# A delta-rule layer's exponentials and powers reordered, pooled sums on zero-padded rows, small parameters loaded one group ahead

## The chip, the cores and the metric

The kernel runs on one core of one Trainium2 chip. The metric is the device time of one execution in microseconds. Engine names in the profile: PE is TensorE (PEld its weight loads), DVE is VectorE, ACT is ScalarE, POOL is GpSimd, SP is SyncE, which here only issues DMAs.

## The reference

A decoder trunk of four pre-norm residual layers on x of 256 tokens by 1024 channels, all in float32, with one last RMSNorm. The layers are, in order: pooling mixer, gated delta rule, latent attention, pooling mixer. What matters here is cut from the reference:

```python
def pool_mixer(h, w_in, w_grp, scale, w_out):            # layers 0 and 3
    u, gate = jnp.split(h @ w_in, 2, axis=-1)            # 2 x 2048 channels
    ...                                                  # groups of 512 channels, windows 2, 4, 8, 16
        mean = (cg[:, 1:] - lo) / cnt                    # causal mean over w tokens, cnt = min(t + 1, w)
        groups.append(mean.astype(u.dtype) - u[..., sl])
    p = jnp.einsum('bsgi,gio->bsgo', p, w_grp)...
    y = p * scale * jax.nn.silu(gate)
    return y @ w_out

def gdn_mixer(h, w_in, conv_w, a_log, dt_bias, norm_g, w_out):   # layer 1
    proj = h @ w_in
    qkv = jax.nn.silu(causal_depthwise_conv(qkv, conv_w))        # 4 taps
    q = l2norm(q) * (GDN_DK ** -0.5);  k = l2norm(k)             # x * rsqrt(sum(x * x) + EPS)
    beta = jax.nn.sigmoid(b_raw)
    g = -jnp.exp(a_log) * jax.nn.softplus(a_raw + dt_bias)
    o = chunk_gated_delta_rule(q, k, v, g, beta)
    o = rmsnorm(o, norm_g) * jax.nn.silu(gate)
    return o @ w_out

def chunk_gated_delta_rule(q, k, v, g, beta):
    g = jnp.cumsum(g, axis=-1)
    decay = jnp.exp(jnp.where(causal, g_i - g_j, -jnp.inf))
    L = jnp.where(strict, (k_beta @ k^T) * decay, 0.0)
    sol = triangular_solve(I + L, [v_beta, k_beta * exp(g)])     # unit lower triangular
    attn = jnp.where(causal, (q @ k^T) * decay, 0.0)
    ...                                                          # a state is carried from chunk to chunk
```

## The kernel before, in words

**Products.** Every large product is made of float32 values split into two parts of fewer bits, a high and a low one: `weights` loads a piece of 128 x 1024 of a weight matrix into one of three buffers `raw` (SP's queue), ScalarE casts it to `whi` (L149, L153) and VectorE subtracts to get `wlo` (L150, L154; a few pieces on GpSimd, by the argument `pool`). Both go to a ring of nine buffers. PE then makes three matmuls (high by high, high by low, low by high) at L162. `project` runs eight k-steps of 128 rows for 512 columns into PSUM banks named `acc` (or `aux`).

**Order of the work.** The program is written in an order by hand, and a planner then orders each engine's queue by due times from its own model of costs. Each engine works through its queue strictly in order, so a step that waits holds everything behind it on that engine. `later(*instructions)` makes the steps traced inside it come after the given instructions on the engine of each of these, and adds no wait between engines. `mark` keeps the last instruction of a kind for that.

**Pool layer** (`pool_layer`, layers 0 and 3). Four groups in the order 3, 2, 1, 0; for each, `gate(g)` and `pooled(g)`; the product with the group's weights, `mixed`, follows one group later. `pooled` brings the projection to a tile `u` (128 channels x 4 x 256 tokens), and then builds window sums by doubling: level `lev` adds a copy shifted by d = 2^lev tokens. The first d columns have no partner and are copied on GpSimd (L552), the rest is a sum on VectorE (L553). L557 corrects the first tokens' counts, L561 forms `p`, and L242 and L247 split it to `ph` and `pl` for `mixed`.

**Small parameters.** After the gates of the first layer's groups 3, 2 and 1 stand `turn_params` with `window_counts`, `gdn_setup` and `mla_setup`. Each loads small parameters on ScalarE's queue and uses them at once: `turn_params` transposes the gains' rows on PE (L489) to `colsT`; `gdn_setup` transposes the convolution's taps (L640, L641) and splits the small weights `bw` to `bws` (L647, L648); `mla_setup` makes the position tables by some twenty small VectorE steps (L1108 on).

**Delta-rule layer** (`gdn_layer`). The order by hand is

```python
order = "g0 k0 d a0 k1 a1 s g1 q0 v0 v1 v2 b q1 i V3 c3 g2 u0 u1 g3".split()
```

where g is a gate's projection (512 columns), k a half of the keys, q a half of the queries, v a quarter of the values, and:

- Before the loop, the cumulated g of each token is made (`G`), turned, written to DRAM and read back to every partition as `Gb` (GpSimd's queue, L730, L733); 16 VectorE steps (L740) form `DT` = min(Gb - G, mask).
- d, `decays`: the exponentials of both halves of `DT`, of `Eb` (= `Gb[1]`) and of `eG` on ScalarE (L748).
- k and q, `channels`: projection, convolution (`conv`: four scalings on ScalarE, L755, and 12 steps on VectorE, L758), silu on ScalarE (L804), transposes on PE (L810), squares on ScalarE (L813), their sum `ssq` on VectorE (L814). `keys` then makes on GpSimd `ssq` + EPS (L841) and `rk`, its power -1/2 (L789), and on VectorE `s1` = rk * beta (L843), `s2` = s1 * rk (L845).
- a, `lower`: k by k^T on PE (L823), times s2 and the decay on VectorE, giving `LT` (L832); diagonal blocks of 32 are copied out (L856, L858).
- s, `substitution`: VectorE turns the blocks (L861), GpSimd solves them by 31 pairs of steps (L867, L871). Also the reciprocal `rki` = 1 / rk (L873), by which the values are scaled (L934).
- b, `blocks_back`: VectorE turns the result (L878), ScalarE and GpSimd copy it to the blocks of `T` (L885, L887), and GpSimd scales the token-wise keys `ktok` (L888).
- i, `inverses`: the 32-blocks are joined to inverses of 64. V3, c3 and u: last values, and the first chunk's new values.
- `queries` ends with a product on VectorE (L902) and, on GpSimd after the last substitution step (mark "blocks"), the powers of the queries' norms (L904 to L908). They are used by `output` (L1060, L1063), `ktok` by `state` (L1029).

ScalarE's functions lie in tables; a change between exponential, logarithm and silu shows in the profile as an ACT_TABLE_LOAD at the line of the next function.

## Time and profile before

| | |
|---|---|
| time, median of 3 runs | 816.21 us (813.97 to 816.85) |
| time of the profiled execution | 817.07 us |
| its span, first to last instruction | 815.4 us |
| mean granted TensorE clock | 0.992 |
| instructions | 16122 |
| GpSimd busy | 148.7 us (18%) |
| read from HBM | 136.74 MB, 169 GB/s over the span |

A row of the profile names the line, the engine, the operation, the tile written and those read (out<-in), the shape and the count. In a timeline the two numbers ahead are the start and the duration in us, and the bracket at the end is the time for which the engine was idle before, and what it waited for. Rows of groups end in the total busy time and the mean duration in ns of one. "Busy" of PE counts pipelined matmuls, so a busy PE need not be at its peak. "Granted clock" is the share of full speed that PE's clock had.

### The profile page before, as it was taken

The numbers are of one execution on the slowest core, as the hardware profiler recorded it, in microseconds if no ns is written. First come the engines' busy times: TensorE is split into PE (matmuls) and PEld (weight loads), VectorE is DVE, ScalarE is ACT, GpSimd is POOL, SyncE is SP. The second block draws the span as 40 slices with busy tenths as digits, with TensorE's granted clock in tenths as the row PEclk, the third lists the DMA queues.
The fourth block names the chain that finished last, engine by engine and source line by source line (L and its number), as shares of the span: only waits on it lengthen the run. The fifth ranks groups of instructions, "written<-read, shape, count | busy, mean of one in ns | idle before, by whom it ended". The sixth has DMA issues, their size and how long they took to land.

```text
span 815.4 us, 16122 instructions
## 1 busy us (share of the span) xinstructions
PE 794.6 (97%) x5966; PEld 754.8 (93%) x5966; DVE 598.6 (73%) x1133; ACT 500.2 (61%) x1009; POOL 148.7 (18%) x292
## 2 busy tenths in 40 slices
PE   8989999999989989999999999999999999999996
PEld 7979999989889988888989999999999989999996
DVE  4699987667889976456677659778877667877863
ACT  6566555567876855455565654566655575566662
POOL 3001100233037852022212013000000210000011
PEclk9999999999999999999999999999999999999999
DMA  6765666746455633323557686753652646676562
GB/s 208 227 177 177 197 214 219 219 154 209 152 161 156 205 113 100 127 73 108 182 148 221 204 191 183 208 145 87 182 172 74 187 153 196 191 222 207 198 213 53
DMA packets 106615, 138.85 MB, mean 170 GB/s; under 512 B 19044, under 2 KB 48936, under 8 KB 106536
## 3 DMA queue, kind: packets, MB, share of 16 engines
q1 hardware_dynamic: 104032, 136.07, 55.2%
q0 software_dynamic: 320, 1.06, 0.4%
q8 instruction: 47, 0.77, 0.4%
q10 hardware_dynamic: 2184, 0.69, 0.4%
q14 instruction: 32, 0.26, 0.1%
HBM read 136.74 MB, written 1.06 MB: 169 GB/s over the span
## 4 chain that ended last, share of the span: by engine, by line
PE 85%; POOL 5%; ACT 3%; DVE 3%; issue 2%; DMA 1%; ACTq 0%; SPq 0%; DVEq 0%; POOLq 0%
PE acc L162 69%; PE aux L162 8%; POOL X L867 2%; POOL U L871 2%; ACT whi L149 1%; PE tp L1337 1%; DVE cv L758 1%; DMA x<-in_x_dram 1%; DVE wlo L150 1%; PE aux L823 1%; ACT junk L256 1%; PE tp L419 0%; PE aux L979 0%; PE aux L961 0%; PE aux L1002 0%
## 5 line engine op out<-in xcount | busy, mean ns | idle before, releaser
L150 DVE TENSOR_TENSOR wlo<-raw,whi 128x512 fp32r<-128x512 f32 (+1 forms) x370 | 250.1, 702 | 98.4 <-ACT whi L149 96.1
L149 ACT CAST whi<-raw 128x512 fp32r<-128x512 f32 (+1 forms) x380 | 223.1, 618 | 156.1 <-PE acc L162 78.9
L162 PE MATMUL acc<-hTl,whi 128*128 128x256 f32 x832 | 230.5, 277 | 0.0
L162 PE MATMUL acc<-hTh,whi 128*128 128x256 f32 x832 | 229.3, 276 | 0.0
L162 PE MATMUL acc<-hTh,wlo 128*128 128x256 f32 x832 | 229.1, 276 | 0.0
L162 PEld LDWEIGHTS acc<-hTl,whi 128*128 128x128 f32 x832 | 160.1, 192 | 0.2
L162 PEld LDWEIGHTS acc<-hTh,whi 128*128 128x128 f32 x832 | 160.0, 192 | 0.3
L162 PEld LDWEIGHTS acc<-hTh,wlo 128*128 128x128 f32 x832 | 159.9, 192 | 0.1
L162 PE MATMUL acc<-wlo,yTh 128*128 128x256 f32 (+1 forms) x384 | 112.3, 311 | 0.0
L162 PE MATMUL acc<-whi,yTh 128*128 128x256 f32 (+1 forms) x384 | 112.3, 315 | 0.0
L162 PE MATMUL acc<-whi,yTl 128*128 128x256 f32 (+1 forms) x384 | 89.1, 313 | 0.0
L162 PEld LDWEIGHTS acc<-wlo,yTh 128*128 128x128 f32 x384 | 73.2, 191 | 3.1
L162 PEld LDWEIGHTS acc<-whi,yTh 128*128 128x128 f32 x384 | 72.9, 191 | 3.1
L162 PEld LDWEIGHTS acc<-whi,yTl 128*128 128x128 f32 x384 | 63.1, 191 | 3.4
L153 ACT ACTIVATE whi<-raw,gain 128x512 fp32r<-128x512 f32 x64 | 43.7, 719 | 31.1 <-DMA raw<-in_pool_w_in_dram 25.6
L153 ACT ACTIVATE whi<-raw,colsT 128x512 fp32r<-128x512 f32 x64 | 44.5, 722 | 29.5 <-DMA raw<-in_pool_w_out_dram 18.1
L154 DVE SCALAR_TENSOR_TENSOR wlo<-raw,colsT,whi 128x512 fp32r<-128x512 f32 x64 | 47.4, 762 | 19.0 <-ACT whi L153 18.4
L162 PE MATMUL acc<-wlo,hTh 128*128 128x512 f32 (+1 forms) x144 | 54.1, 381 | 0.4 <-DVE wlo L150 0.2
L154 DVE SCALAR_TENSOR_TENSOR wlo<-raw,gain,whi 128x512 fp32r<-128x512 f32 x64 | 46.2, 743 | 10.0 <-ACT whi L153 7.5
L162 PE MATMUL acc<-whi,hTh 128*128 128x512 f32 (+1 forms) x144 | 52.8, 379 | 0.7 <-ACT hTh L242 0.7
L387 POOL TENSOR_TENSOR hg<-x,gain 128x256 f32<-128x256 f32 x16 | 13.4, 846 | 208.3 <-DVE x L451 208.3
L162 PE MATMUL acc<-whi,hTl 128*128 128x512 f32 (+1 forms) x144 | 42.5, 373 | 0.0
(368 smaller groups left out, 1526.2 us busy)
## 6 DMA issues: line engine op xcount, KB each, us to landing
raw<-in_pool_w_in_dram SPq DMA_DIRECT2D x62, 512.0 KB, 4.6
raw<-in_gdn_w_in_dram SPq DMA_DIRECT2D x48, 512.0 KB, 3.9
raw<-in_pool_w_out_dram SPq DMA_DIRECT2D x32, 512.0 KB, 4.6
raw<-in_mla_w_in_dram SPq DMA_DIRECT2D x24, 512.0 KB, 4.5
raw<-in_mla_w_uq_dram SPq DMA_DIRECT2D x36, 256.0 KB, 3.6
raw<-in_pool_w_grp_dram SPq DMA_DIRECT2D x16, 512.0 KB, 3.8
raw<-in_gdn_w_out_dram SPq DMA_DIRECT2D x16, 512.0 KB, 3.5
raw<-in_mla_w_ukv_dram SPq DMA_DIRECT2D x32, 256.0 KB, 3.4
```

Source lines behind the costliest of these rows:

```text
L149: a = nc.scalar.copy(hi, v)
L150: b = e.tensor_tensor(out=lo, in0=v, in1=hi.bitcast(F32), op=ALU.subtract)
L153: a = nc.scalar.activation(hi, v, AF.Copy, scale=g)
L154: b = e.scalar_tensor_tensor(out=lo, in0=v, scalar=g, in1=hi.bitcast(F32), op0=ALU.mult, op1=ALU.subtract)
L162: return nc.tensor.matmul(inorder(o, n), lhsT=lhs, rhs=woven(rhs, n), start=start, stop=stop)
L256: nc.scalar.activation(junk[:, :n], src, AF.Square, scale=scale, accum_out=o)
L387: nc.gpsimd.tensor_tensor(out=self.early[t, a], in0=xs[t][:, sl], in1=self.g[:, sl], op=ALU.mult)
L758: mark["conv"] = nc.vector.scalar_tensor_tensor(out=o[:, d:], in0=ps[:, :S - d], scalar=tp(3 - d, c), in1=o[:, d:], op0=ALU.mult, op1=ALU. ...
L823: nc.tensor.matmul(ps[:, b], lhsT=kT[hf][:, b, tt], rhs=rhs[hf][:, b, tt], start=True, stop=True)
L867: nc.gpsimd.tensor_tensor(out=pv, op=ALU.mult, in0=Lb[:, r + 1:, r:r + 1].to_broadcast([P, n, c]), in1=Tb[:, r:r + 1, :c].to_broadcast([P, ...
L871: mark["blocks"] = nc.gpsimd.tensor_tensor(out=tv, in0=tv, in1=pv, op=ALU.subtract).ins
L1337: nc.tensor.transpose(ps[:, a * P:(a + 1) * P], sb[:, a * P:(a + 1) * P], ident)
```

## The change

- **Parameters.** `turn_params`, `gdn_setup` and `mla_setup` now only issue their loads (and steps that need none) and return a function `finish` with the steps that use what was loaded. The pool layer calls it one group later. The loads stand where they stood.
- **Pooled sums.** `u` and the sums get 16 columns in front, which hold zeros for `u` (a memset on GpSimd). A level adds cur[a:] and cur[a - d : -d], from column a = 16 - w + 2d on, so that the copies on GpSimd fall away.
- **Exponentials.** `eG` is made right after `G`. The `DT` steps move from before the loop into `decays`, which comes after the last convolution step on VectorE and the last silu on ScalarE so far (new mark "silu"), that is those of k0, and no longer after the last gate's silu.
- **Norms.** For the keys, VectorE adds EPS, takes the reciprocal and multiplies by beta, which is s2; GpSimd makes `rki` as the power +1/2. `rk` and `s1` go. The powers of the queries' norms, for both halves, and the scaling of `ktok` move to a new step `query_norms`, "n", behind i, on GpSimd after the copies of `blocks_back` (new mark "back").
- **Order.** q0 comes before g1 instead of after it.

```diff
+        def finish():                       # turn_params
+            ps = bank(tps, "tp")
+            nc.tensor.transpose(ps[:, :P], rows, ident)
+            nc.vector.tensor_copy(colsT, ps[:, :P])
+        return [finish]
...
-            u = big("u", 4, S)
+            before = WINDOWS[-1]
+            padded = big("u", 4, before + S)
+            u = padded[:, :, before:]
+            nc.gpsimd.memset(padded[:, :, :before], 0.0)
...
-            cur = u
+            cur = padded
             for lev in range(g + 1):
                 d = 1 << lev
-                nxt = big("win", 4, S)
-                nc.gpsimd.tensor_copy(nxt[:, :, :d], cur[:, :, :d])
-                nc.vector.tensor_tensor(out=nxt[:, :, d:], in0=cur[:, :, d:],
-                                        in1=cur[:, :, :S - d], op=ALU.add)
+                a = before - w + 2 * d
+                nxt = big("win", 4, before + S)
+                nc.vector.tensor_tensor(out=nxt[:, :, a:], in0=cur[:, :, a:],
+                                        in1=cur[:, :, a - d:-d], op=ALU.add)
                 cur = nxt
+            cur = cur[:, :, before:]
...
-            if not place:
-                with later(*[m for k, m in mark.items() if k not in ("rest", "strip", "conv")]):
-                    turn_params()
-                    window_counts()
-            elif setups:
-                with later(*[m for k, m in mark.items() if k not in ("rest", "strip", "conv")]):
-                    setups.pop(0)()
+            if lead:
+                with later(*[m for k, m in mark.items() if k != "rest" and k != "strip"]):
+                    if not place:
+                        window_counts()
+                    for finish in loaded:
+                        finish()
+                    loaded = setups.pop(0)() if setups else []
...
+        def finish():                       # gdn_setup
+            ps = bank(tps, "tp")
+            nc.tensor.transpose(ps[:, :P], crow, ident)
+            nc.vector.tensor_copy(tap, ps[:, :P])
+            nc.vector.tensor_copy(bws[:, :, 0, :], bw)
+            nc.vector.tensor_tensor(out=bws[:, :, 1, :], in0=bw, op=ALU.subtract,
+                                    in1=bws.bitcast(F32)[:, :, 0, :])
+        return [finish]
...
-        order = "g0 k0 d a0 k1 a1 s g1 q0 v0 v1 v2 b q1 i V3 c3 g2 u0 u1 g3".split()
+        order = "g0 k0 d a0 k1 a1 s q0 g1 v0 v1 v2 b q1 i n V3 c3 g2 u0 u1 g3".split()
...
+        nc.scalar.activation(eG, G, AF.Exp)
...
-        for t in range(NT):
-            for h in range(H):
-                nc.vector.scalar_tensor_tensor(out=DT[t][:, h, :], in0=Gb[t][:, h, :],
-                                               scalar=G[:, t, h:h + 1], in1=maskT,
-                                               op0=ALU.subtract, op1=ALU.min)
         def decays():
-            with later(*[m for n, m in mark.items() if n == "gate"]):
-                for a in (*DT, Eb, eG):
-                    nc.scalar.activation(a, G if a is eG else a, AF.Exp)
+            with later(mark["conv"], mark["silu"]):
+                for t in range(NT):
+                    for h in range(H):
+                        nc.vector.scalar_tensor_tensor(out=DT[t][:, h, :], in0=Gb[t][:, h, :],
+                                                       scalar=G[:, t, h:h + 1], in1=maskT,
+                                                       op0=ALU.subtract, op1=ALU.min)
+                for a in (*DT, Eb):
+                    nc.scalar.activation(a, a, AF.Exp)
...
         def keys(hf):
             hs = slice(4 * hf, 4 * hf + 4)
             channels(kT, GDN_QK, hf, 0)
-            nc.gpsimd.tensor_scalar(ssq[:, 0, :, hs], ssq[:, 0, :, hs], EPS, None, ALU.add)
-            power(rk[:, :, hs], ssq[:, 0, :, hs])
-            nc.vector.tensor_tensor(out=s1[:, :, hs], in0=rk[:, :, hs], in1=beta[:, :, hs],
-                                    op=ALU.mult)
-            nc.vector.tensor_tensor(out=s2[:, :, hs], in0=s1[:, :, hs], in1=rk[:, :, hs],
-                                    op=ALU.mult)
+            n, r = ssq[:, 0, :, hs], s2[:, :, hs]
+            nc.vector.tensor_scalar(n, n, EPS, None, ALU.add)
+            nc.vector.reciprocal(r, n)
+            nc.vector.tensor_tensor(out=r, in0=r, in1=beta[:, :, hs], op=ALU.mult)
+            nc.gpsimd.tensor_tensor(out=rki[:, :, hs], in0=n, in1=half[:, 1], op=ALU.pow)
...
-            nc.vector.reciprocal(rki, rk)
...
-            nc.gpsimd.tensor_tensor(out=ktok, in0=ktok, op=ALU.mult,
-                                    in1=DT[0][:, :, P - 1:].to_broadcast([P, H, P]))
...
-            with later(mark["blocks"]):
-                nc.gpsimd.tensor_scalar(qh, ssq[:, 1, :, 4 * hf:4 * hf + 4], float(P), EPS * P,
-                                        ALU.mult, ALU.add)
-                power(rh, qh)
-                nc.gpsimd.tensor_tensor(out=qh, in0=rh, in1=rh, op=ALU.mult)
-                nc.gpsimd.tensor_scalar(qh, qh, 1.0 / DV, None, ALU.mult)
+        def query_norms():
+            with later(mark["back"]):
+                nc.gpsimd.tensor_scalar(rq2, ssq[:, 1], float(P), EPS * P, ALU.mult, ALU.add)
+                for hf in range(2):
+                    hs = slice(4 * hf, 4 * hf + 4)
+                    nc.gpsimd.tensor_tensor(out=rq[:, :, hs], in0=rq2[:, :, hs], in1=half[:, 0],
+                                            op=ALU.pow)
+                nc.gpsimd.tensor_tensor(out=rq2, in0=rq, in1=rq, op=ALU.mult)
+                nc.gpsimd.tensor_scalar(rq2, rq2, 1.0 / DV, None, ALU.mult)
+                nc.gpsimd.tensor_tensor(out=ktok, in0=ktok, op=ALU.mult,
+                                        in1=DT[0][:, :, P - 1:].to_broadcast([P, H, P]))
...
-        MC["rope"] = rope_tables()          # mla_setup: now the loads of posi stand here,
+        def finish():                       # and the tables are made by
+            MC["rope"] = rope_tables(posi)
+        return [finish]
...
-    setups = [gdn_setup, mla_setup][:max(0, depth - 1)]
+    setups = [turn_params, *(gdn_setup, mla_setup)[:max(0, depth - 1)]]
```

More of the change, by code (lines that the diff above doesn't have):

```diff
@@ L487, in turn_params @@
             at += n
-        ps = bank(tps, "tp")
-        nc.tensor.transpose(ps[:, :P], rows, ident)
-        nc.vector.tensor_copy(colsT, ps[:, :P])
+        def finish():
[3 more added lines that the diff above has]
+        return [finish]
     def col(name, i):
@@ L625, in gdn_setup @@
             nc.gpsimd.memset(m32[64 * a + 32:64 * a + 64, a], 1.0)
-        half = const.tile([P, NT, GDN_H // 2], F32, name="halves")
-        nc.gpsimd.memset(half, -0.5)
+        half = const.tile([P, 2, NT, GDN_H // 2], F32, name="halves")
+        for a in range(2):
+            nc.gpsimd.memset(half[:, a], a - 0.5)
         cols = workb("cols", 2, 32)
@@ L638, in gdn_setup @@
         tap = const.tile([P, P], F32, name="tap")
-        ps = bank(tps, "tp")
-        nc.tensor.transpose(ps[:, :P], crow, ident)
-        nc.vector.tensor_copy(tap, ps[:, :P])
         bw = workb("bw", KD, 16)
@@ L646, in gdn_setup @@
             "(k p) c -> p k c", p=P))
-        nc.vector.tensor_copy(bws[:, :, 0, :], bw)
-        nc.vector.tensor_tensor(out=bws[:, :, 1, :], in0=bw, in1=bws.bitcast(F32)[:, :, 0, :],
-                                op=ALU.subtract)
         alog = const.tile([P, GDN_H], F32, name="alog")
@@ L783, in gdn_layer @@
         ssq = small("ssq", 2, NT, H, bufs=1)
-        rk, rki, rq, rq2, s1, s2 = (
-            sc(n) for n in ("rk", "rki", "rq", "rq2", "s1", "s2"))
+        rki, rq, rq2, s2 = (sc(n) for n in ("rki", "rq", "rq2", "s2"))
         neG = small("neG", H, bufs=1)
-        def power(o, a):
-            nc.gpsimd.tensor_tensor(out=o, in0=a, in1=half, op=ALU.pow)
         def channels(dst, c0, hf, which):
@@ L803, in channels @@
                         o, v = halves(o), parted(v)
-                    nc.scalar.activation(o, v, AF.Silu)
+                    mark["silu"] = nc.scalar.activation(o, v, AF.Silu).ins
             for c in range(0, 4, 2):
@@ L886, in blocks_back @@
                 else:
-                    nc.gpsimd.tensor_copy(o, tv[dd])
-            nc.gpsimd.tensor_tensor(out=ktok, in0=ktok, op=ALU.mult,
-                                    in1=DT[0][:, :, P - 1:].to_broadcast([P, H, P]))
+                    mark["back"] = nc.gpsimd.tensor_copy(o, tv[dd]).ins
         at_ = []
@@ L1011, in gdn_layer @@
                  "c": values_done}
-        once = {"s": substitution, "d": decays, "b": blocks_back, "i": inverses}
+        once = {"s": substitution, "d": decays, "b": blocks_back, "i": inverses,
+                "n": query_norms}
         for name in order:
@@ L1100, in rope_tables @@
             nc.gpsimd.memset(inv[:, a:a + 1], float(10000.0 ** (-a / HALF)))
-        posi = const.tile([P, NT], I32, name="posi")
-        for b in range(2):
-            nc.scalar.dma_start(out=posi[b * 64:(b + 1) * 64],
-                                in_=positions[0].rearrange("(t a b) -> b a t", t=NT, b=2)[b])
         cs = const.tile([P, NT, 2, HALF], F32, name="cs")
@@ L1138, in mla_setup @@
     def mla_setup():
-        MC["rope"] = rope_tables()
+        posi = const.tile([P, NT], I32, name="posi")
+        for b in range(2):
+            nc.scalar.dma_start(out=posi[b * 64:(b + 1) * 64],
+                                in_=positions[0].rearrange("(t a b) -> b a t", t=NT, b=2)[b])
         cmask = small("cmask", P, bufs=1)
```

7 lines of the change are left out of this document (3 added, 4 removed).

## The prediction

> **What bounds the kernel now.** The page's busy shares come first: they name the engine whose idle time is the price list.
>
> ```profile
> span 815.4 us, 16122 instructions
> ...
> PE 794.6 (97%) x5966; PEld 754.8 (93%) x5966; DVE 598.6 (73%) x1133; ACT 500.2 (61%) x1009; POOL 148.7 (18%) x292
> ```
>
> PE's stream of matmuls is the time: 97% of the span, and the change takes no matmul away. So a gain can only be PE's idle time and what that drags behind it. Second view, what PE waited for (us in total, times, longest), and then the four waits in the timeline, with the idle time before each in brackets:
>
> ```profile
> PE tp L810 <- ACT kqT L804: 7.2, 3, 3.4
> PE acc L162 <- ACT ph L242: 2.8, 1, 2.8
> ```
>
> ```profile
> 57.03 0.48 PE L162 MATMUL acc<-whi,ph 128*128 128x512 f32 x1 [2.77 <-ACT ph L242]
> ...
> 209.84 0.44 PE L810 MATMUL tp<-ident,kqT 128*128 128x128 f32 x2 [1.26 <-ACT kqT L804]
> ...
> 228.58 0.69 PE L810 MATMUL tp<-ident,kqT 128*128 128x128 f32 x2 [3.35 <-ACT kqT L804]
> ...
> 294.78 0.44 PE L810 MATMUL tp<-ident,kqT 128*128 128x128 f32 x2 [2.63 <-ACT kqT L804]
> ```
>
> They hold 10.0 us: one for the first pool group's p, three for the silus of keys and queries in the delta-rule layer. Third view, busy time by stretch; the columns to read are PE, DVE, POOL and the granted clock, the third number from the end:
>
> ```profile
> 50.00:60.00 10.00, 7.15 (x47) 6.03 (x46) 9.75 (x16) 8.31 (x12) 0.00 (x0) 0.89 0.67 207
> 60.00:70.00 10.00, 10.00 (x70) 9.34 (x69) 10.00 (x14) 5.65 (x8) 4.06 (x3) 0.94 0.55 160
> 200.00:210.00 10.00, 8.74 (x64) 8.08 (x63) 8.17 (x24) 8.48 (x13) 2.19 (x4) 1.00 0.67 224
> 220.00:230.00 10.00, 6.65 (x54) 6.46 (x54) 9.29 (x25) 5.46 (x11) 1.91 (x4) 0.92 0.75 210
> 230.00:240.00 10.00, 10.00 (x83) 10.00 (x82) 6.83 (x14) 7.64 (x18) 4.53 (x3) 0.90 0.51 158
> 290.00:300.00 10.00, 7.37 (x54) 7.18 (x53) 9.28 (x17) 7.96 (x16) 5.36 (x7) 0.84 0.37 108
> 300.00:310.00 10.00, 10.00 (x83) 9.68 (x83) 9.27 (x18) 4.66 (x11) 3.35 (x4) 0.99 0.33 105
> 190.00:300.00 110.00, 102.75 (x844) 100.72 (x844) 94.14 (x202) 80.85 (x159) 56.22 (x92) 0.97 0.56 168
> ```
>
> Three of the four waits are followed by a lower clock. 0.89 and 0.94 in two stretches of 10 us lose 1.1 + 0.6 = 1.7 us of full-speed time, 0.92 and 0.90 lose 1.8, 0.84 and 0.99 lose 1.7. The wait of 1.26 is followed by none. So a wait of 2.6 us or more costs itself and about 1.7 us, and the whole price list is 10.0 + 5.2 = 15.2 us.
>
> **Place 1, the first pool group.**
>
> ```profile
> 40.70 0.23 DVE L647 CAST bws<-bw 128x128 fp32r<-128x128 f32 x1 [2.63 <-DMA bw<-in_gdn_w_in_dram]
> ...
> 54.31 1.22 DVE L561 SCALAR_TENSOR_TENSOR p<-win,u 128x1024 f32<-128x1024 f32 x1
> ```
>
> VectorE stood 2.63 us for bw, a parameter of the next layer, with this group's window sums queued behind the wait; shortly before p it was full (9.75 of 10 us). The change moves the cast, its subtraction, the tap copy and a transpose one group later. Their DMAs, the gains' and the positions' stay in their groups on ScalarE's queue, so no transfer moves past another and SP's queue has no part in it. The 2.63 us and three small steps like the 0.23 of the cast, 0.7 together, leave the way to p: 3.3 us, against PE's wait of 2.77. I take the wait and its dip as gone: 2.8 + 1.7 = **4.5 us**. Bounds: 0, if the weights' own DMAs hold VectorE as long as the parameter did, and 4.5; the upper end, because the wait removed is longer than PE's. The steps that are moved, and the position tables (from the third group to the last), lie beside matmuls for which PE does not wait; without that cover they would cost about 0.7 us there.
>
> **The padded sums.**
>
> ```profile
> L552 POOL COPY win<-win x12: 204/572/1712, 42.9 to 731.8; 128x8 f32<-128x8 f32 x6, 128x16 f32<-128x16 f32 x4, 128x32 f32<-128x32 f32 x2
> ...
> L552 POOL COPY win<-u x8: 220/472/1783, 37.3 to 756.7; 128x4 f32<-128x4 f32 x8
> L553 DVE TENSOR_TENSOR win<-u x8: 1212/1214/1217, 41.5 to 756.8; 128x1020 f32<-128x1020 f32 x8
> ```
>
> Twenty GpSimd copies go, 12 with a median of 0.57 us and 8 with 0.47. They run beside VectorE's sum of the same level (1.21), so I cost them at nothing. Eight memsets of 64 columns come instead, on an engine that is 18% busy; a memset may wait there for its buffer, with nothing urgent queued behind it in a pool layer. The sums become longer: in the widest group 1080, 1072, 1056 and 1024 elements for 1020, 1016, 1008 and 992. At 1.2 ns for an element (1214 ns by 1020) that is 0.24 us on the way to p and about 0.35 us in a layer: hidden in seven groups, and in the first by the 0.5 us that place 1 has to spare. The tiles of u and the sums grow from 4096 to 4352 bytes in a partition; the trace shows no wait for a buffer at these lines, so that is costed at nothing, with 0.5 us as an upper end.
>
> **Place 2, the first keys' silus and the exponentials.**
>
> ```profile
> 203.81 2.19 DVE L740 SCALAR_TENSOR_TENSOR DT<-Gb,G,maskT 128x128 f32<-128x128 f32 x8 [1.83 <-DMA Gb<-d_g]
> 205.92 0.47 DVE L758 SCALAR_TENSOR_TENSOR cv<-acc,tap,cv 128x253 f32<-128x253 f32 x1
> ...
> L748 ACT ACT_TABLE_LOAD x3 | 3.8, 1283 | 0.1
> L804 ACT ACT_TABLE_LOAD x3 | 3.8, 1283 | 0.1
> ```
>
> The last convolution step of the first keys stood behind the wait for Gb (1.83) and eight DT rows (2.19), so its silu fell among the exponentials, with a table load on either side. With decays() behind the last convolution step and silu of k0, that step comes 4.0 us sooner and the four silus run together. The 16 DT rows and three exponentials follow; nothing needs them before the LT rows. PE's 1.26 us go: **1.3 us**. Of the six loads at these two lines four stay (eG, silu, exponentials, silu): 2 x 1.28 = 2.6 us less on ScalarE. What waits now: DT for Gb's landing, with weight splits queued behind on VectorE as before; the exponentials for DT, with the second keys' convolution queued behind on ScalarE.
>
> **Place 3, the second keys.**
>
> ```profile
> 226.81 1.28 ACT L804 ACT_TABLE_LOAD   x1
> ```
>
> This load stays, and the silus behind it end PE's wait of 3.35. ScalarE has 2.6 us less to do ahead of them, so they come up to 2.6 sooner; PE arrives 1.3 sooner itself (place 2), and the wait shrinks by 1.3, to about 2.1. Whether the dip of 1.8 goes with a wait of 2.1 no row says (1.26 had none, 2.63 had one), so I count half of it: 1.3 + 0.9 = **2.2 us**; bounds 0 and 3.4 + 1.8 = 5.2. q0 comes before g1 now: both are projections over 8 k-steps, so PE's cover for the keys is the same, but q0's convolution moves one projection nearer (rival e).
>
> **Place 4, the norms and the substitution.**
>
> ```profile
> 233.38 1.92 POOL L888 TENSOR_TENSOR ktok<-ktok,DT 128x1024 f32<-128x1024 f32 x1 [5.56 <-issue]
> 235.38 0.57 POOL L841 TENSOR_SCALAR ssq<-ssq 128x8 f32<-128x8 f32 x1
> 236.04 2.04 POOL L789 TENSOR_TENSOR rk<-ssq,halves 128x8 f32<-128x8 f32 x1
> ...
> 239.29 0.16 DVE L845 TENSOR_TENSOR s<-s,rk 128x8 f32<-128x8 f32 x1
> ...
> 288.84 1.07 DVE L878 STREAM_TRANSPOSE U<-U 128x512 f32<-128x512 f32 x1 [3.85 <-POOL U L871]
> ```
>
> GpSimd's substitution ends so late that VectorE stands 3.85 us for it with the queries' convolution queued behind, and then PE for those queries. It starts from LT rows that need s2, and s2 came by GpSimd: ktok's product (1.92), eps (0.57), the power (2.04), then VectorE's product at 239.29. Now VectorE does add, reciprocal and product itself, three steps like the 0.16 of L845; GpSimd's power makes only rki, which the values need later; ktok and the queries' powers go behind the copies back (step n). That takes 4.5 us of GpSimd from in front of the second LT rows and adds 0.5 us of VectorE. The substitution starts about 4 us sooner against PE's work; PE's wait is 2.63. I take it and its dip as gone: 2.6 + 1.7 = **4.3 us**; bounds 0 and 4.3. Step n puts two powers, some small steps and ktok on GpSimd, 2 x 2.04 + 1.92 + 1 = 7 us, behind q1's norms and ahead of its share of the later gates' splits. GpSimd was busy 3.35 of 10 us there, so it is covered; if not, up to 4 us of late splits, with PE behind them.
>
> **The sum:** 4.5 + 1.3 + 2.2 + 4.3 = 12.3 us. The profiled execution took 817.1 us (span 815.4), 0.9 above the median of the three runs, 816.2. From its own time 804.8 come out, on the scale of the median 803.9.
>
> **The rivals.** (a) VectorE is the real bound of the delta-rule stage. For it: 94.14 busy of 110 us from 190 to 300; with 7.8 us of places 2 to 4 gone it would have to be 92% busy. Against it: 9.75 and 10.0 of 10 us occur in the pool layer. Then places 3 and 4 give nothing: 816.2 - 5.8 = 810.4. (b) Place 1 stays, by its lower bound: 816.2 - 7.8 = 808.4. (c) The dips do not hang on these waits but come at their own times. For it: 1.26 had none. Against it: the three others each had one, and nowhere else in the table is the clock low without a wait. Then 1.7 + 0.9 + 1.7 come off the sum: 808.2. (d) The change does not do what it says: the planner, which writes every engine's order anew from its own costs, lays waits of the same size elsewhere: 816.2, give or take 4. (e) Slower: q0's convolution, 12 steps like the 0.47 at 205.92, comes ahead of the second LT rows on VectorE, now that q0 stands before g1. The substitution starts 5.6 us later than now, PE's wait at its end grows by as much, and q0's transposes wait as k1's do, 3.4 + 1.8. Less the 5.8 us of places 1 and 2 that is +5.0: 821.2. It decides from a delay of 10 us in both together; the direct s2 speaks against it.
>
> [...]
>
> **How the numbers follow.** My forecast 0.54 (own range 800 to 808), (a) 0.18, (b) 0.06, (c) 0.04, (d) 0.11, (e) 0.07. Predicted: 804. The range goes down to 799.5 (all of the 15.2, and 1.5 for small waits) and up to 812 (place 1 alone, 816.2 - 4.5, is 811.7). Half a per cent is 4.1 us, about what a measurement of this kernel can tell from no change: faster 0.54 + 0.18 + 0.06 + 0.04 = 0.82, same 0.11, slower 0.07.
>
> **What would show it.** Place 1: no VectorE wait for bw ahead of p, and a clock of 1.00 from 50 to 70 us. Place 2: four silus under one load, PE without a wait near 208. Place 3: a wait of PE for k1's silus of about 2 us. Place 4: s2 with no GpSimd step before it, and VectorE's transpose at the substitution's end without a wait. The prediction is wrong if PE's waits for L804 still add up to 5 us or more, or if a new line appears among PE's waits.

## The result, and the profile after

The changed kernel takes 811.44 us in the median of 8 runs (810.1 to 814.1), beside 815.99 for the kernel before in the same series (813.97 to 817.62): a ratio of 0.9943, 95% interval 0.9924 to 0.9962. That is 4.6 us, not the 12 of the forecast. A second series on another chip gave 812.29 beside 818.41, a ratio of 0.9916 (0.9890 to 0.9942); the medians are 6.1 us apart, and the ratio stands for 6.9. The direction and the range held; the size did not.

The page after, span and busy times:

```profile
span 812.4 us, 16075 instructions
...
PE 795.3 (98%) x5966; PEld 754.5 (93%) x5966; DVE 601.3 (74%) x1134; ACT 498.6 (61%) x1007; POOL 132.7 (16%) x276
```

What PE waited for (total, times, longest):

```profile
PE tp L819 <- ACT kqT L813: 3.6, 2, 1.9
...
PE tp L593 <- DVE y L587: 0.9, 1, 0.9
PE acc L162 <- ACT ph L242: 0.7, 1, 0.7
...
PE acc L162 <- DVE wlo L154: 0.7, 2, 0.4
PE acc L162 <- DVE pl L247: 0.3, 1, 0.3
```

L813 and L819 are the old L804 and L810. The four waits of before were 10.0 us; these rows add up to 6.2: 3.8 us are gone, where the forecast had 8.0 (2.8 + 1.3 + 1.3 + 2.6; the rest of the 12.3 were low clocks). The stretches in the timeline, in the same columns as before:

```profile
50.00:60.00 10.00, 8.93 (x61) 7.94 (x60) 9.59 (x15) 7.61 (x12) 0.00 (x0) 1.00 0.65 196
220.00:230.00 10.00, 9.87 (x62) 8.64 (x61) 7.91 (x20) 9.93 (x24) 2.25 (x4) 1.00 0.60 177
240.00:250.00 10.00, 8.11 (x73) 8.03 (x73) 9.70 (x19) 7.65 (x16) 8.67 (x18) 1.00 0.62 180
280.00:290.00 10.00, 8.34 (x75) 8.15 (x74) 7.69 (x11) 8.04 (x16) 5.91 (x5) 1.00 0.24 73
290.00:300.00 10.00, 9.96 (x62) 9.96 (x63) 7.66 (x15) 3.33 (x7) 1.28 (x1) 0.66 0.58 181
190.00:300.00 110.00, 106.13 (x873) 103.79 (x872) 98.37 (x205) 78.43 (x158) 54.40 (x87) 0.97 0.56 171
```

The waits at 57, 208 and 228 us are gone or small. One is new at 240 (q0's silu, PE 8.11 of 10), and the one for q1 near 290 is still there (8.34), followed by a clock of 0.66: two low stretches of 3.41 us, 3.4 us lost.

For the kernels on which the argument rests, a ledger: by how much later (+) or sooner PE issues the same matmul, counted from the first, than in the profiled execution of before, gained or lost in each stretch (borders in the time of before). A low window is 3.41 us between 50 and 800 us at a granted clock of 0.50, as the traces of before and after show each of theirs, and costs 1.7 us (half of it); before has three (one ahead of 86 us, two in the delta-rule stretch). Each row is one execution.

| profiled execution | 0 to 45 us | to 86 | to 192 | to 325 (delta rule) | rest | low windows |
|---|---|---|---|---|---|---|
| after | +0.6 | -3.1 | +1.2 | -2.9 | +1.1 | 2 |
| after, again | +1.5 | -2.5 | +1.5 | -6.2 | 0.0 | 0 |
| parameters alone | +1.7 | -3.0 | +1.4 | +2.1 | 0.0 | 3 |
| after, tables early | +1.0 | -3.3 | +5.2 | -6.5 | 0.0 | 1 |
| sums alone | +1.2 | -1.1 | +0.2 | +1.9 | 0.0 | 2 |
| delta-rule part alone | +0.3 | +0.2 | 0.0 | -5.3 | +0.1 | 1 |
| exponentials alone | -0.4 | -0.2 | 0.0 | +1.1 | 0.0 | 4 |
| norms alone | +0.6 | +0.1 | 0.0 | -3.4 | +0.2 | 2 |
| order s g1 q0 | +1.9 | -3.1 | +1.5 | -5.2 | +3.6 | 1 |
| fourth tap left out | +2.0 | -2.8 | +1.8 | -5.3 | +4.8 | 1 |
| four raw buffers | +0.7 | -5.0 | +0.4 | -3.6 | +0.4 | 2 |
| copies back behind q1 | +0.8 | -2.7 | +1.4 | -5.7 | +1.5 | 1 |
| both of these | +1.4 | -5.0 | +0.7 | -9.7 | +0.1 | 0 |
| both, without parameters and sums | +1.7 | -5.0 | +0.3 | -8.9 | +1.8 | 1 |
| delta-rule part alone, four buffers | +0.9 | -5.0 | +0.4 | -3.6 | +0.4 | 2 |
| before, four buffers | +6.4 | -5.0 | +1.7 | +6.5 | +12.8 | 5 |

The first column moves by up to 2 us, most of it ahead of 15 us, with the start of full clock: it begins at 10.0 us in the execution of before, at 11.4 in that of after and at 13.0 when it was run again; in the first two a 128x512 matmul of L162 takes 0.63 us at 9.5 us and 0.38 at 14. (The 6.4 us of the last row are mostly waits, at 16 and 33 us.)

### The profile page after: what moved, and what is told of

The parts are those of the page before. It is cut to its first block, busy times and chain, and to the rows that moved or that the text cites. A ratio compares the mean times of both kernels' runs of the same rounds, so it can differ in the third digit from the quotient of the medians.

```text
span 812.4 us, 16075 instructions
## 1 busy us (share of the span) xinstructions
PE 795.3 (98%) x5966; PEld 754.5 (93%) x5966; DVE 601.3 (74%) x1134; ACT 498.6 (61%) x1007; POOL 132.7 (16%) x276
## 4 chain that ended last, share of the span: by engine, by line
PE 72%; DMA 8%; DVE 7%; POOL 5%; issue 4%; ACT 3%; ACTq 0%; SPq 0%; DVEq 0%
PE acc L162 57%; PE aux L162 7%; DMA raw<-in_pool_w_in_dram 3%; POOL U L879 2%; POOL X L875 2%; DMA raw<-in_gdn_w_in_dram 2%; DVE wlo L150 2%; DVE wlo L154 1%; DVE win L560 1%; ACT whi L153 1%; DMA Gb<-d_g 1%; ACT whi L149 1%; PE tp L1351 1%; DMA raw<-in_pool_w_out_dram 1%; DMA x<-in_x_dram 1%
## 5 line engine op out<-in xcount | busy, mean ns | idle before, releaser
L150 DVE TENSOR_TENSOR wlo<-raw,whi 128x512 fp32r<-128x512 f32 (+1 forms) x370 | 252.0, 707 | 100.7 <-ACT whi L149 98.6
L162 PE MATMUL acc<-hTl,whi 128*128 128x256 f32 x832 | 231.4, 278 | 0.0
L162 PE MATMUL acc<-hTh,whi 128*128 128x256 f32 x832 | 229.9, 277 | 0.0
L162 PE MATMUL acc<-hTh,wlo 128*128 128x256 f32 x832 | 229.9, 277 | 0.0
L162 PEld LDWEIGHTS acc<-hTl,whi 128*128 128x128 f32 x832 | 160.6, 193 | 0.2
L162 PEld LDWEIGHTS acc<-hTh,whi 128*128 128x128 f32 x832 | 160.4, 193 | 0.3
L162 PEld LDWEIGHTS acc<-hTh,wlo 128*128 128x128 f32 x832 | 160.5, 193 | 0.1
L162 PE MATMUL acc<-wlo,yTh 128*128 128x256 f32 (+1 forms) x384 | 112.2, 311 | 0.7 <-DVE wlo L154 0.7
L162 PE MATMUL acc<-whi,yTh 128*128 128x256 f32 (+1 forms) x384 | 112.0, 315 | 0.0
L162 PE MATMUL acc<-whi,yTl 128*128 128x256 f32 (+1 forms) x384 | 89.0, 313 | 0.0
L162 PEld LDWEIGHTS acc<-wlo,yTh 128*128 128x128 f32 x384 | 73.2, 191 | 4.5 <-DVE wlo L154 1.5
L162 PEld LDWEIGHTS acc<-whi,yTh 128*128 128x128 f32 x384 | 72.9, 191 | 3.1
L162 PEld LDWEIGHTS acc<-whi,yTl 128*128 128x128 f32 x384 | 63.0, 191 | 3.3
L154 DVE SCALAR_TENSOR_TENSOR wlo<-raw,colsT,whi 128x512 fp32r<-128x512 f32 x64 | 47.4, 767 | 18.6 <-ACT whi L153 18.1
L154 DVE SCALAR_TENSOR_TENSOR wlo<-raw,gain,whi 128x512 fp32r<-128x512 f32 x64 | 46.2, 744 | 13.0 <-ACT whi L153 11.3
L162 PE MATMUL acc<-wlo,hTh 128*128 128x512 f32 (+1 forms) x144 | 54.4, 383 | 0.4
L162 PE MATMUL acc<-whi,hTh 128*128 128x512 f32 (+1 forms) x144 | 53.1, 381 | 0.7 <-ACT hTh L242 0.7
L162 PE MATMUL acc<-whi,hTl 128*128 128x512 f32 (+1 forms) x144 | 42.5, 373 | 0.0
```

The lines of the kernel that those rows point to most:

```text
L150: b = e.tensor_tensor(out=lo, in0=v, in1=hi.bitcast(F32), op=ALU.subtract)
L154: b = e.scalar_tensor_tensor(out=lo, in0=v, scalar=g, in1=hi.bitcast(F32), op0=ALU.mult, op1=ALU.subtract)
L162: return nc.tensor.matmul(inorder(o, n), lhsT=lhs, rhs=woven(rhs, n), start=start, stop=stop)
```

## The parts one by one

**Each part alone on the kernel before** (the hunks of the diff for the parameters, for the sums, and for the delta-rule layer).

> The kernel before with the parameters' part alone. Ledger theory (each part costs and gains at its own place, as the two traces read): the wait of PE for the first pool group's p (2.8 us and its lower clock, 1.7) shrinks to about 1 us without a dip, -3.3; the position tables in the last pool group make PE wait for late weight splits, +1.2; the delta-rule layer is as before. Sum -2.1: 813.9 by a median before of 816.0. Rival (the order of the planner shifts by chance, and the parts do not add up): no wait near 118 to 126 us, or changes of over 1 us in the delta-rule layer; anything from 812 to 817.

> The kernel before with the padded window sums alone. Ledger theory: 0 in the first layer (the wait for bw still holds p), and PE waits some 1 us for y near 706 us in the second pool layer, where the sums are 0.03 us longer each: 816 to 817. Rival (that wait is the pace of the weights' DMAs in one execution, not the sums): no wait near 706 us in this profile, 816. If the copies on GpSimd had held p after all, PE's wait near 57 us would shrink, and the time would fall to 813 to 815.

> The kernel before with all of the delta-rule layer's part. Ledger theory: PE's waits near 209 and 228 us and the dip go (-6.6), a wait of 2.1 for the first queries' silu comes near 242 us, the wait for the second queries' silu stays at 1.9 with a dip of two windows (-0.9 + 1.7): about -3.5, 812.5; the first pool group is as before with 2.8 us of wait and its dip. Rival (the planner's order by chance): the waits of the layer fall at other places or have other sizes than in the changed kernel's trace.

Measured ratios: parameters 0.9994 (0.9974 to 1.0014), sums 0.9994 (0.9973 to 1.0015), delta-rule part 0.9926 (0.9901 to 0.9951). So, by time, the delta-rule part gives the gain of the whole change. PE's waits in it are 2.1 us for q0 and 1.9 for q1, as its theory had them, but with no low window behind them. The parameters do shorten the wait at 57 us in the trace, from 2.8 to 0.7 us, but PE then waits for weight splits of a later group (0.5 us at 119 us), and the delta-rule stretch got 2.1 us worse in that execution, one more low window (1.7) among them. With the sums alone no wait near 706 us showed, so the sums alone don't make the wait of 0.9 in the changed kernel; it was missing, too, when that kernel was profiled again.

**The position tables.** They run as some twenty VectorE steps at 95 to 114 us now, ahead of the waits near 118.

```diff
-        def finish():
-            MC["rope"] = rope_tables(posi)
-        return [finish]
+        MC["rope"] = rope_tables(posi)
+        return []
```

> The changed kernel with the position tables made at once in the third group, as before, all other parameters one group later. Ledger theory: PE's two waits for weight splits near 118 and 121 us go, -1.2 us: 810.2. Rival (the last group is late for another reason, the longer sums or the weights' DMAs): the waits near 118 and 121 us stay and the time is 811.4.

0.9960 (0.9937 to 0.9984): no faster than the changed kernel, and PE's waits from 116 to 121 us grew to 2.7 us in three pieces. The tables' place is not their cause.

**The two halves of the delta-rule part**, exponentials (`decays`, `eG`, mark "silu") and norms (s2 on VectorE, powers and `ktok` in "n"), each alone on before, with g1 ahead of q0.

> Kernel of before with the exponentials' part alone: decays and exponentials behind the first keys' last convolution step and silu, eG ahead; norms, their powers on GpSimd and the order s g1 q0 as before. Theory (places 2 and 3 are the exponentials' doing): PE's waits near 208 and 228 are gone with the dip at 228, place 4 keeps its wait of about 2.6 us for q1's silu because the substitution still starts from GpSimd's powers: 4 to 6 us faster than before, and no wait near 241 for q0, because g1 stands ahead of it. Rival (the gain needs the norms too, since VectorE frees s2 and ScalarE's loads alone do nothing): 1.3 us faster at most, and the wait near 228 stays above 2 us.

> Kernel of before with the norms' part alone: s2 on VectorE, the queries' powers and ktok's product behind the copies back; exponentials and the order s g1 q0 as before. Theory (the substitution's end is earlier but VectorE's queue then sets q1's silu): the waits near 208 and 228 stay (1.3 and 3.4 us with a dip), VectorE's transpose at the substitution's end waits under 1.5 us, PE still waits 1 to 2 us for q1's silu: 0 to 2 us faster than before. Rival (the prediction's place 4): the wait near 294 and its dip are gone, 4.3 us faster.

Exponentials 1.0001 (0.9980 to 1.0023), norms 0.9944 (0.9926 to 0.9961). With the exponentials alone the theory falls; the rival has the time, but not its wait near 228. With the norms alone the theory falls too: the ratio stands for 4.6 us (3.2 to 6.1), what the rival, the prediction's place 4, expected, though its wait is shorter and not gone. PE's waits with the exponentials alone, and PE's and VectorE's rows at place 4:

```profile
PE tp L810 <- ACT kqT L804: 6.9, 3, 5.8
```

```profile
281.70 1.07 DVE L878 STREAM_TRANSPOSE U<-U 128x512 f32<-128x512 f32 x1 [5.20 <-POOL U L871]
```

```profile
294.14 0.69 PE L810 MATMUL tp<-ident,kqT 128*128 128x128 f32 x2 [5.76 <-ACT kqT L804]
```

The waits at 208 and 228 (1.3 and 3.4 before) shrink to 1.1 together, and PE stands at place 4 at 288.4 instead of 292.2. But the queries come at 294.1 instead of 294.8, so what was won is waited out there, 5.8 us, with three low windows from 293.2 us on. With the norms alone that end moves: the waits there are 0.5 and 1.3 us, while those of places 2 and 3 are 2.4 and 1.1. All four:

```profile
PE tp L807 <- ACT kqT L801: 5.2, 4, 2.4
```

Places 2 and 3 are thus worth nothing where place 4 doesn't move; whether they add to it isn't settled (0.9926 for the whole delta-rule part, 0.9944 for the norms, and the intervals overlap). They are not terms to be added.

## Place 4 and the new wait

VectorE after the substitution in the changed kernel, then ScalarE, GpSimd and PE in the same stretch:

```profile
278.82 1.07 DVE L885 STREAM_TRANSPOSE U<-U 128x512 f32<-128x512 f32 x1 [1.50 <-POOL U L879]
279.82 0.65 DVE L150 TENSOR_TENSOR wlo<-raw,whi 128x512 fp32r<-128x512 f32 x1
282.78 2.27 DVE L150 TENSOR_TENSOR wlo<-raw,whi 128x512 fp32r<-128x512 f32 x1 [2.31 <-ACT whi L149]
284.97 0.47 DVE L771 SCALAR_TENSOR_TENSOR cv<-acc,tap,cv 128x255 f32<-128x255 f32 x1
...
286.36 2.35 DVE L961 STREAM_TRANSPOSE U<-T 128x1024 f32<-128x1024 f32 x2
```

```profile
279.93 2.18 ACT L892 COPY T<-U 32x512 f32<-32x512 f32 x2 [1.77 <-DVE U L885]
282.13 0.62 ACT L149 CAST whi<-raw 128x512 fp32r<-128x512 f32 x1
282.66 0.83 ACT L768 ACTIVATE cv<-acc,tap 128x256 f32<-128x256 f32 x2
```

```profile
282.59 1.91 POOL L916 TENSOR_TENSOR ktok<-ktok,DT 128x1024 f32<-128x1024 f32 x1
```

```profile
290.04 0.44 PE L819 MATMUL tp<-ident,kqT 128*128 128x128 f32 x2 [1.70 <-ACT kqT L813]
```

and the step of before that followed its transpose (288.84):

```profile
289.83 0.44 DVE L758 SCALAR_TENSOR_TENSOR cv<-acc,tap,cv 128x255 f32<-128x255 f32 x1
```

The substitution is done 10 us sooner (transpose at 278.82 for 288.84). But q1's first convolution step came 1.0 us behind that transpose before, and 6.2 now. Between stand a wait of 2.31 for a whi that ScalarE has behind T's copies (2.18), a split of 2.27 beside ktok's product, and further on the two transposes of T, 2.35.

The new wait, q0's, on ScalarE, PE and in SP's queue (from 190 to 300 us):

```profile
237.45 0.62 ACT L149 CAST whi<-raw 128x512 fp32r<-128x512 f32 x1 [3.35 <-DMA raw<-in_gdn_w_in_dram]
...
240.44 1.14 ACT L149 CAST whi<-raw 128x512 fp32r<-128x512 f32 x2 [1.46 <-DMA raw<-in_gdn_w_in_dram]
241.48 0.43 ACT L813 ACTIVATE kqT<-cv 128x256 f32<-128x256 f32 x1
```

```profile
241.97 0.44 PE L819 MATMUL tp<-ident,kqT 128*128 128x128 f32 x2 [1.90 <-ACT kqT L813]
```

```profile
SPq L133 <- DVE wlo L150: 47.4, 16, 7.6
```

The silu stands on ScalarE behind casts that wait for weights; the weights' DMA waits on SP's queue for one of three buffers, which VectorE's split frees late. Five kernels take away one piece each of these two queues.

```diff
-        order = "... s q0 g1 v0 v1 v2 b q1 i n ..."        # order
+        order = "... s g1 q0 v0 v1 v2 b q1 i n ..."
```

> The changed kernel with the second gate group ahead of the first queries again (s g1 q0, as before the change). Theory (VectorE's work from 200 to 300 sets the time and PE's waits only tell where it is paid): the wait for q0's silu near 241 goes, but one for k1's near 225 or a longer one for q1's near 290 comes, within 1.5 us of the changed kernel. Rival (the order of q0 and g1 is what makes that wait): 2 us or more faster than the changed kernel, with the waits for q1 as before at 1.9.

0.9970 (0.9954 to 0.9986), 816.5 us, where the changed kernel took 812.3 in the same series. q0's wait goes; instead PE waits 0.4 us at 227, 0.6 at 275 and 2.5 at 289. In the ledger the delta-rule stretch is as good as the changed kernel's, but 3.5 us are lost near 650 us, in a layer that the edit doesn't touch: the planner laid casts and splits there otherwise. Neither side had that.

```diff
-                nc.gpsimd.tensor_tensor(out=ktok, ...)      # ktok's product, in query_norms
+            with later(mark["conv"]):
+                nc.gpsimd.tensor_tensor(out=ktok, ...)
```

> The changed kernel with ktok's product on GpSimd held back until q1's last convolution step, so that it doesn't run beside the splits that VectorE makes ahead of that convolution (one wlo took 2.27 us beside it, the others 0.68). Theory (the two engines hold each other up, and this is on the way to q1's silu): that wlo takes 0.68 us again, the silu comes 1.6 us sooner, PE's wait of 1.9 shrinks to about 0.3: 1.6 to 3.5 us faster than the changed kernel. Rival (the wlo waits for something else, or the time is lost a little later when ktok's product runs beside other VectorE work): within 0.5 us of it.

```profile
284.91 0.69 DVE L150 TENSOR_TENSOR wlo<-raw,whi 128x512 fp32r<-128x512 f32 x1 [2.33 <-ACT whi L149]
```

The same split takes 0.69 with no product beside it, so the 2.27 were ktok's; in the changed kernel it ended 0.6 us behind the product. The planner put the product not later but to 227.7 us, ahead of the second rki: `later` orders only on the engine of the given instruction, here VectorE, so the edit took the product from behind the copies back and held it to nothing on GpSimd. PE waited 0.6 and 2.2 us for q0, and 0.6 for q1. 0.9933 (0.9909 to 0.9957): the same. What the split saves isn't seen in the time; whether the product costs q0 as much at its new place isn't shown. In the trace of the changed kernel the 289 splits of 128x512 at L150 that VectorE makes with no GpSimd step beside them take 0.67 to 0.75 us; the one of 2.27 has the product beside it for 1.72. At the new place VectorE's EPS step for the keys (L851, 128x8) takes 1.58 beside the product, where it is 0.16 and 0.17 in the changed kernel.

```diff
-                with later(mark["strip"], mark["dve" if name == "i" else "conv"]):   # inverses
+                with later(mark["strip"], mark["conv"]):
```

> The changed kernel with the inverses held back until q1's last convolution step, so that the two big transposes of T (2.35 us of VectorE) no longer stand ahead of that convolution. Theory (VectorE's queue ahead of q1's convolution sets PE's wait of 1.9 us at 288): the silu of q1 comes 2.3 us sooner, the wait and the low clock behind it are gone: 2 to 4 us faster than the changed kernel, some 807.5 to 809.5 where that takes 811.4. Rival (those 2.35 us of VectorE are needed soon after, so PE waits for the inverses' copies instead, or for wlo): 811 or slower, with a new wait behind 290.

810.4 us, 0.9926 (0.9900 to 0.9951). PE's waits for q1 fell to 0.5 and 0.8 us, and the one for q0 was 1.5, with a low window; in time it is between the two series of the changed kernel, which doesn't decide.

```diff
-                for d in range(1, 4):                       # convolution's steps
+                for d in range(1, 4 if c >= 16 else 3):
```

> The changed kernel with the fourth tap of the keys' and queries' convolutions left out (sixteen VectorE steps of about 0.47 us, 7.5 us less for VectorE between 200 and 290; nothing less for the other engines, so its keys and queries lack that term). Theory (VectorE bounds the delta-rule stage): both waits of about 2 us shrink under 1 us each and the stage ends 3 to 6 us sooner: 806 to 809 where the changed kernel takes 811.4. Rival (DMA and buffers pace it, or the planner's order does): the waits stay, within 1.5 us of the changed kernel.

816.4 us, 0.9967 (0.9947 to 0.9986), where the changed kernel took 812.3 in the same series, with 6.9 us less of convolution steps on VectorE (14.2 for 21.1). The loss isn't in this stretch: the ledger has 4.8 us lost behind 325 us, part of it near 655 us as with the order above, and from 192 to 325 us as much won as in the changed kernel. In the stretch:

```profile
190.00:300.00 110.00, 104.72 (x874) 102.44 (x873) 94.17 (x193) 80.14 (x162) 53.19 (x87) 0.98 0.56 170
```

VectorE is less busy, 94.2 of 110, and PE too: 104.7. The wait for q0 is gone, but there are 2.7 us at 215 (k1) and 2.1 at 292 (q1), against the theory. So VectorE's total work isn't what bounds this stretch.

```diff
-    rawp = ctx.enter_context(tc.tile_pool(name="rawp", bufs=3))
+    rawp = ctx.enter_context(tc.tile_pool(name="rawp", bufs=4))
```

> The changed kernel with four raw weight buffers in place of three. The wait for q0's silu stands behind a whi that waits 3.35 and 1.46 us for its raw weights, whose DMA waits on SP's queue for a buffer that VectorE's late split frees. Theory A (this loop is what makes q0's wait): the whi's waits and PE's wait near 241 go, about 2 us faster. Theory B (VectorE has the work to do in any case): the DMAs come earlier but the silus do not, or the wait moves to q1: within 1 us of the changed kernel.

810.2 us, 0.9895 (0.9876 to 0.9915). q0's wait is gone and so is the one at 57 us; PE reaches q1 at 283.4 and waits there for 3.9:

```profile
287.27 0.44 PE L819 MATMUL tp<-ident,kqT 128*128 128x128 f32 x2 [3.85 <-ACT kqT L813]
```

ScalarE's waits for raw weights from 190 to 300 us, in the changed kernel and with four buffers:

```profile
ACT whi L149 <- DMA raw<-in_gdn_w_in_dram: 17.4, 9, 4.1
```

```profile
ACT whi L149 <- DMA raw<-in_gdn_w_in_dram: 1.7, 2, 1.1
```

So the loop of buffer, DMA and split made q0's wait (theory A), and q1's queue is a second, separate one. What was won at q0 is waited out at q1, as theory B had it: in the ledger the delta-rule stretch is no better than the changed kernel's, and the gain, 2.1 us beside 812.3 in this series, is at 57 us.

**The changed kernel once more.**

> The changed kernel once more, nothing edited: another execution to set beside the first. Theory (low clock comes in windows of 3.41 us on a grid that starts at another phase in each execution, and a wait of about 2 us costs such a window or two in one execution and none in the next): the waits for q0's and q1's silus are there again within 0.6 us of 2.1 and 1.9, but the low windows stand elsewhere or there are fewer than two. Rival (a low window belongs to its wait): the double window behind the wait near 288 is there again.

```profile
PE tp L819 <- ACT kqT L813: 4.2, 3, 2.0
```

```profile
280.00:290.00 10.00, 9.36 (x84) 9.16 (x83) 7.68 (x12) 7.92 (x15) 5.97 (x5) 1.00 0.35 104
290.00:300.00 10.00, 8.44 (x78) 8.25 (x79) 8.29 (x17) 4.74 (x11) 1.28 (x1) 1.00 0.53 168
```

The same two silus are waited for, 4.2 us in all, q1's in two pieces of 0.9 and 1.3, and there is no low clock up to 800 us. So whether a wait brings a low window changes from one execution to the next; with the sums alone a wait of 2.7 us near 58 us had none either.

## Both causes taken away, and what four buffers need

```diff
-        order = "... v0 v1 v2 b q1 i n ..."                 # copies back behind q1
+        order = "... v0 v1 v2 q1 b i n ..."
```

> The changed kernel with the copies back (b: VectorE's transpose at the substitution's end, T's copies) behind the second queries' projection and convolution, order v0 v1 v2 q1 b i n. Theory (place 4 wasn't gained because what follows the substitution's end stands ahead of q1's convolution: VectorE's wait of 2.31 us for a whi that ScalarE puts behind T's copies, a split of 2.27 us beside ktok's product, and the two transposes of T, 2.35): q1's silu comes 4 to 6 us sooner, PE's wait near 289 is gone, the wait for q0's near 241 stays: 2 to 3.5 us faster than the changed kernel, which took 812.3 on the last chip. Rival (the inverses come later by as much, and PE waits for them): within 1 us of the changed kernel, with a new PE wait between 295 and 330.

> The changed kernel with both: four raw weight buffers, and the copies back behind q1. Theory (the two waits that stayed have these two causes, and they are independent): no wait of PE above 1 us between 50 and 300, clock without a low window there: 5 to 7 us faster than the changed kernel, 805 to 807. Rival (VectorE's total work in the stage bounds it, so one wait gone is paid at the next): about what four buffers gave alone, 2 us.

> The changed kernel with four raw buffers and the inverses behind q1's convolution, the copies back left where they are. With four buffers alone PE waited 3.9 us for q1's silu. Theory (the two transposes of T are part of that queue): that wait falls by about 2.3 to 1.6, 1 to 3.5 us faster than four buffers alone and 1 to 3 us slower than with the copies back moved. Rival (the substitution's end alone sets q1's silu): the wait stays at 3.9, no faster than four buffers alone.

> The kernel of before with four raw weight buffers in place of three, nothing else. Theory (the buffers free place 1, which the small parameters alone did only in part, while the waits of the delta-rule layer hang on GpSimd's norms and stay): the wait near 57 and its low clock are gone, those near 208, 228 and 294 stay: 2 to 5 us faster than before. Rival (buffers help only the changed kernel, whose order made q0's wait): within 1 us of before.

Copies back behind q1 (the inverses and ktok's product need them and move too): 0.9929 (0.9903 to 0.9956), the rival's time. q1's wait is gone, q0's is left, and PE waits for values at 305 us instead, which it doesn't with four buffers:

```profile
PE tp L819 <- ACT kqT L813: 1.9, 1, 1.9
PE tp L940 <- ACT vc L936: 1.7, 1, 1.7
```

With four buffers as well (both diffs): **804.63 us, 0.9836 (0.9818 to 0.9853)**, below both kernels. Its largest wait behind 50 us, and its delta-rule stretch:

```profile
PE aux L994 <- DVE X L991: 0.8, 1, 0.8
```

```profile
190.00:300.00 110.00, 110.00 (x918) 107.79 (x916) 104.84 (x218) 83.65 (x167) 62.77 (x93) 1.00 0.56 174
```

PE shows no idle time in this stretch, and VectorE is 95% busy and not in its way. Four buffers with the inverses' diff gave 0.9887 (0.9870 to 0.9905), with q1's wait at 2.6 us for 3.9: T's transposes are a part of that queue, the copies back and what hangs on them the larger one.

Four buffers alone on the kernel before made it slower: 839.07 us, 1.0260 (1.0242 to 1.0278). That was on neither side. The ledger has 6.4 us lost up to 45 us; the wait at 57 goes there too (5.0 us won to 86 us); but the planner orders the rest anew, and PE waits for convolutions in the delta-rule layer, and in small pieces until 660 us:

```profile
PE acc L162 <- DVE cv L758: 6.3, 2, 5.9
```

Last, the two versions with four buffers without parameters and sums:

> The kernel of before with the delta-rule part and four raw buffers, without the padded sums and the earlier parameters. Four buffers made the kernel before 2.6% slower, with waits behind the late copies of the convolution, a late row of parameters near 33 us and many small ones after 300, and the changed kernel faster. Theory (the early waits there, 6 us up to 50 us, are the parameters that are loaded and used in one group, and the rest is the delta-rule layer's old order): the early loss stays at about 6 us, from 190 to 330 the stage is within 2 us of the changed kernel's with four buffers; 813 to 817 in all. Rival (the delta-rule part alone turns the four buffers into a gain): 810 or faster.

> The fastest kernel so far (four raw buffers, copies back behind q1) without the padded sums and the earlier parameters. Theory (the two parts that were worth nothing by themselves carry some 6 us once the weights run ahead): 810 to 813, with PE's waits near 17 and 33 us and none from 200 to 300. Rival (they are worth nothing here too): 804 to 806.

0.9915 (0.9886 to 0.9944) and 0.9851 (0.9820 to 0.9882): within the intervals the same as with these parts (0.9895 and 0.9836). My theory that they pay where the weights run ahead falls. It is the delta-rule part with which four buffers no longer cost anything; that they gain with it alone isn't shown (0.9915 for 0.9926). Why the planner's order for the old layer loses so much with them stays open.

## Why the prediction was wrong

- **Place 4** (forecast 4.3 of 12.3) is the step that failed. What it rests on held: s2 came without GpSimd, and the substitution was done 10 us sooner, 5 to 6 against PE's work, where 4 were expected (VectorE's transpose still waited 1.5 us, of 3.85). But "I take it and its dip as gone" did not come true: PE waits 1.7 and 2.2 us for q1's silu in the two profiles of the changed kernel, where it was 2.6, with two low windows in one and none in the other. The step took the substitution's end for the only thing ahead of that silu. What stands between the two is a queue of its own, 6.2 us from the transpose to q1's convolution where it was 1.0, and step n, costed at nothing, put ktok's product into it. With the norms alone the time fell by 4.6 us (0.9944), all that place 4 was to give; with the earlier places PE comes to q1 sooner, and waits out a part of their gain there. So the four places don't add up. Taking that queue and the late weights away together gave the rest of the forecast's time: 13.0 us between the medians, and in the ledger 5.0 up to 86 us and 9.7 in the delta-rule stretch, where the forecast had 4.5 and 7.8.
- **q0 ahead of g1** was seen as a danger (rival e), but by its convolution and at 5 us. It came as 1.9 to 2.1 us by ScalarE's queue and the raw buffers; the run with g1 first and the four-buffer run show it.
- **Place 1** (4.5) is the other term that was far too large: by itself the part measured 0.5 us (-1.1 to 2.1). VectorE's wait for bw went, but with the later start taken off p came 2.4 us sooner, not 3.3, and PE still waits 0.7 to 1.4 us. Of the ledger's 2.5 to 3.1 us, 1.2 to 1.5 are given back by 192 us, most of it from 118 to 126, where PE waits for splits: the steps that were moved did not keep the cover that the prediction counted on, and without which it priced them at 0.7. With four buffers PE's wait goes wholly, although VectorE stands for bw as before (the delta-rule part and four buffers, below). ScalarE's casts waited 8.2 us for raw weights from 30 to 60 us in before and 0.5 there. So the wait for p hung on the weights as well, the reason named for its lower bound.

```profile
38.20 0.23 DVE L648 CAST bws<-bw 128x128 fp32r<-128x128 f32 x1 [2.51 <-DMA bw<-in_gdn_w_in_dram]
```

- **Places 2 and 3** happened: no wait near 208, two table loads fewer (four at L736, L761 and L813, below), the wait at 228 gone rather than shrunk to 2.1. They were added as if independent of place 4, and the exponentials alone are worth nothing (1.0001).

```profile
L813 ACT ACT_TABLE_LOAD x2 | 2.6, 1283 | 0.0
...
L736 ACT ACT_TABLE_LOAD x1 | 1.3, 1283 | 0.0
L761 ACT ACT_TABLE_LOAD x1 | 1.3, 1283 | 0.0
```

- **The low clocks** (forecast 4.3 saved). 1.7 us for one is right. Tying each to its wait is not: rival (c) had half the truth. The mean granted clock was 0.9928 for before (95 runs of the later series) and 0.9961 for the changed kernel (14 runs of both series); 0.0033 of 812 us is an estimate of 2.7 us saved. With the 3.4 to 3.8 us of waits (6.6 are left in the second profile) that is about 6, and the two series measured 4.6 and 6.1 between the medians.
- **Padded sums** at nothing: held.
- **Rival (a)**, VectorE as the bound, came nearest with 810.4, but its reason falls: with fewer taps VectorE did less and two waits of over 2 us stayed, and at 104.8 of 110 us PE still didn't wait. Rival (d), that the planner lays waits elsewhere, had a part: the order and the taps lost 3.6 and 4.8 us behind 325 us, in steps that those edits don't touch.
- Of the signs named, waits for keys and queries stayed under 5 us, and new lines did appear among PE's waits (y L587, wlo L154).

## What to carry to other kernels

Before adding up the waits that a change removes, follow the last of them to the next thing that is late: waits along one chain pay only if the last one moves, and what stands between a faster producer and its consumer has to be read on every engine's queue. When a wait ends in a cast that waits for its DMA, look at who frees the buffer; what one more buffer is worth hangs on the order (7.4 us won with the copies back behind q1, 2.1 in the changed kernel, 21 lost in the kernel before), so measure it on both. A part of a change that only shortens a wait in the trace should be timed alone before it is credited.

## What the hardware showed unasked

The low clock comes in windows of 3.41 us on a grid whose phase differs between executions: in the profile before they begin at 57.83, 228.50 and 296.76 us, 50 and 20 windows of 3.413 apart, each at a granted clock of 0.50; in that of after two in a row, also at 0.50, begin at 291.25, 68.4 windows from 57.83. In the twenty profiled executions, from 14 to 800 us, a window at full clock in which PE stood idle for 1.93 us or more was followed by a low one in 17 of 17 cases. From 1.42 to 1.92 it was 7 of 15. Below that there were three, all in or ahead of the small matmuls of the inverses (322 to 343 us). So a wait of 2.7 us that fell across a border, 1.2 us of idle time in one window and 1.7 in the next, cost no clock (sums alone, near 58 us), and one of 1.7 us inside a window did (after, at 290). In before and after the idle times that a low window followed are 2.61, 3.27 and 1.43 us of 3.41, and 1.70; the 1.89 us in the window from 240.05 (after) brought none. So in these two traces a part of a window without work was enough, and between 1.4 and 1.9 us the idle time alone doesn't tell.
